# Two attention layers as steps of scores, transposes and products, with half projections between and SBUF shared out by phase

## The chip, the cores and the metric

The kernel runs on one core of a Trainium2 chip. The metric is device time in microseconds for one execution; the time before is the median of three runs, 1935.61 us (1925.61 to 1938.24). Lower is better.

## The reference, cut to what matters

Two trunk layers act on 512 latent tokens and 256 context tokens of width 1024, all in float32:

```python
for i in range(DEPTH):                       # DEPTH = 2
    h_l, h_c = modulate(rms_norm(x)), modulate(rms_norm(ctx))
    if kind == 0: y_l, y_c = diff_attention_mixer(h_l, h_c, ...)   # layer 0, 8 heads
    if kind == 1: y_l, y_c = neighbourhood_mixer(h_l, h_c, ...)    # layer 1, 16 heads
    x = x + mod_l[2] * y_l
    x = x + mod_l[5] * squared_relu_mlp(modulate(rms_norm(x)), w1, w2)
    # ctx likewise in layer 0 alone
```

Layer 0 is differential attention: per head two softmaxes over all keys are formed, the second is subtracted times lambda, and the result weighs the values; its output is normalised per head. Layer 1 is neighbourhood attention: a query sees the 256 context keys and a window of the grid, with a learned position bias added to the window's scores. Queries and keys are normalised per head; in layer 0 the latents also get a rotary embedding. The scales and shifts of each norm come from products of two conditioning vectors with a 1024 x 6144 matrix per layer ("modulation").

## The kernel before, in words

A token tile is 128 tokens; tiles 0 and 1 are context, 2 to 5 latents. A float32 matrix product is made of three passes over split operands (high and low part), each a matmul on float32r; every weight slice is therefore loaded raw (tag R, 2 buffers), copied to its high part by ScalarE (L99) and split by a subtraction on GpSimd (L100) into a W tile. `wload` does this (L90).

The program is a set of Python generators, each a stream of instructions that yields between steps. `run` (L796) steps them in the order that a string of letters gives: `q` projections, `a` the attention of the head before, `b` that of the head that is being projected, `l` and `m` load and compute one of 48 modulation chunks, a capital runs a stream to its end. What the strings give is the order in which instructions are written down; a scheduler in the framework then sets each engine's final order from its own estimate of times, taking earlier-written work first among what is ready.

Layer 0 (heads 1 to 7 in a loop of `hybrid_block`): `load_qkv` fetches four W tiles of the head; `qkv0` makes for each of six token tiles 24 matmuls of 384 columns into a PSUM tile PA (`qkv_matmul`, L346), normalises queries and keys (`qk_normed`: ScalarE copy and square, DVE reduction L358, epsilon added by `rstd` L231, power on GpSimd L233, DVE multiply L361), applies the rotary tables on GpSimd (L406 to L416), and after each pair of tiles transposes them (`turn`, L424, tile PC) and splits them (`q_split`, `k_split`; L385 is a DVE copy of the low key part to the other partition half). `attend0` then goes through the six query tiles. Per tile: scores into a three-bank PSUM tile PS (L458), maximum (L463), exponent (L464), the difference of the two softmaxes (L470), transposes of the weights into PB tiles (L478), high and low parts in an X tile (ScalarE L480, DVE L481), twelve products with the values (L485), the head norm (L488 to L494), and the transpose of the output (L446) one tile late. All of one query tile is one step of the stream.

PSUM in layer 0's attention holds PC once, PB twice, PA twice and PS once; in layer 1 PB twice, PS and PA three times. SBUF pools live for the whole program: W has 5 slots of 8 KB per partition, N has 4 of 4 KB, Y 7 of 1 KB. A head's four weight tiles and the next head's share the 5 slots of W.

Layer 1 has eight groups of two heads: `bias1` loads the position bias (six DMAs of 128 KB into an X tile, L514) and adds the mask on GpSimd (L517), `qkv1` projects, `attend1` makes four units per group (scores L575, bias L578, softmax L581 to L586, a copy of a straddling block L589, transposes L602, splits L603 and L604, products L612).

After each attention, `project` multiplies by the output matrix (L651); the first half of its columns goes beside the last head's attention. The MLPs (`mlp`: L719 up, L728 square, L730 and L731 split, L753 down, L764 sums) run after that.

## Time and profile before

| | before |
|---|---|
| median of 3 runs | 1935.61 us (1925.61 to 1938.24) |
| span of the profiled execution, first to last instruction | 1928.0 us |
| TensorE matmul (PE) busy | 1809.4 us, 94% |
| VectorE (DVE) busy | 1205.3 us, 63% |
| ScalarE (ACT) busy | 812.5 us, 42% |
| GpSimd (POOL) busy | 770.6 us, 40% |
| mean granted TensorE clock | 0.977 |
| HBM traffic | 95 GB/s over the span |

The profile is of one execution; its own total time is not recorded apart from the span, which lies 7.6 us under the median. PE is the row to read first, but matmuls overlap each other in the record, so "busy" also counts stretched matmuls: the spacing of matmuls in dense stretches tells more than the busy share. Waits are listed by who ended them. The stages can be told by their lines: layer 0's heads from about 92 to 445 us, its output projection to 560, its MLP to 1130, layer 1's groups from 1165 to 1490, its projection to 1560, its MLP to the end.

### The profile page before, as it was taken

The page shows a single profiled execution, that of the slowest core. Times are in us where ns is not written, and L with a number is a line of the kernel's source. Part 1 is how long each engine was busy: PE and PEld are TensorE (multiplying, and loading weights), DVE is VectorE, ACT ScalarE, POOL GpSimd, SP SyncE. Part 2 cuts the span into 40 slices and gives each one's busy share as a digit, 9 for nine tenths or more (in the row PEclk, how much of TensorE's full clock was granted, in tenths as well). Part 3 has the DMA queues.
Part 4 walks back from the last instruction along what each step waited for, and adds up shares of the span by engine and source line. Part 5 has one row for each costly group of instructions (what it writes and reads, how often), then busy time and mean ns, then how long its engine had stood idle before and what let it go on. Part 6 is the DMA issues. An engine that isn't in the chain of part 4 may idle for free.

```text
span 1928.0 us, 27111 instructions
## 1 busy us (share of the span) xinstructions
PE 1809.4 (94%) x10256; PEld 1574.1 (82%) x10256; DVE 1205.3 (63%) x2349; ACT 812.5 (42%) x1819; POOL 770.6 (40%) x620
## 2 busy tenths in 40 slices
PE   6899999997899999999999988998998989999998
PEld 5788888885688888888888968998897778888886
DVE  4688888887664343343334685988889664444447
ACT  4466666666342221221221244666656342232231
POOL 3655555544222221221222443444543334344443
PEclk9999999998999999999999998999998999999999
DMA  7222222225222332332432241223323223323331
GB/s 296 92 67 71 86 85 74 73 69 195 84 89 90 118 120 91 128 124 95 131 113 74 57 125 41 50 62 74 77 72 99 93 77 100 97 87 94 103 94 71
DMA packets 58723, 185.02 MB, mean 96 GB/s; under 512 B 7328, under 2 KB 13792, under 8 KB 54496
## 3 DMA queue, kind: packets, MB, share of 16 engines
q1 hardware_dynamic: 52848, 173.44, 29.1%
q10 hardware_dynamic: 5744, 9.85, 1.4%
q8 instruction: 80, 1.31, 0.3%
q14 instruction: 51, 0.42, 0.1%
HBM read 174.45 MB, written 8.81 MB: 95 GB/s over the span
## 4 chain that ended last, share of the span: by engine, by line
PE 67%; DVE 15%; DMA 6%; ACT 4%; POOL 4%; issue 4%; SPq 1%; ACTq 0%; POOLq 0%; DVEq 0%
PE PD L719 23%; PE PA L753 11%; PE PB L753 10%; PE PA L346 9%; PE PA L651 4%; PE PA L200 2%; DMA X<-in_rpb_dram 2%; PE PS L458 2%; PE PB L485 1%; POOL W L100 1%; PE PQ L335 1%; DVE SA L581 1%; DMA N<-oT 1%; DMA R<-in_wmod_dram 1%; DVE N L604 1%
## 5 line engine op out<-in xcount | busy, mean ns | idle before, releaser
L100 POOL TENSOR_TENSOR W<-R,W 128x1024 fp32r<-128x1024 f32 (+1 forms) x200 | 451.0, 2262 | 700.8 <-ACT W L99 700.7
L99 ACT ACTIVATE W<-R 128x1024 fp32r<-128x1024 f32 (+1 forms) x204 | 200.9, 994 | 457.8 <-PE PB L753 364.2
L719 PE MATMUL PD<-Q,W 128*128 128x384 f32 (+1 forms) x1584 | 291.4, 332 | 1.1 <-DVE Q L270 0.5
L719 PEld LDWEIGHTS PD<-Q,W 128*128 128x128 f32 x1584 | 269.5, 188 | 16.6 <-issue 7.0
L346 PE MATMUL PA<-W,H 128*128 128x384 f32 x1008 | 201.8, 347 | 5.1 <-DVE T L209 4.4
L728 DVE TENSOR_TENSOR N<-N 128x768 f32<-128x768 f32 (+1 forms) x64 | 61.9, 969 | 220.3 <-ACT N L727 110.7
L346 PE MATMUL PA<-W,Q 128*128 128x384 f32 (+1 forms) x1008 | 186.7, 332 | 10.9 <-DVE H L535 5.6
L719 PE MATMUL PD<-H,W 128*128 128x512 f32 (+1 forms) x816 | 187.6, 386 | 3.4 <-DVE H L271 2.5
L346 PEld LDWEIGHTS PA<-W,H 128*128 128x128 f32 x1008 | 176.3, 191 | 13.0 <-DVE T L209 4.9
L719 PEld LDWEIGHTS PD<-H,W 128*128 128x128 f32 x816 | 148.9, 191 | 36.3 <-DVE H L271 2.7
L346 PEld LDWEIGHTS PA<-W,Q 128*128 128x128 f32 x1008 | 162.7, 198 | 13.3 <-DVE H L535 7.0
L753 PE MATMUL PA<-W,H 128*128 128x512 f32 x648 | 168.1, 399 | 2.7 <-DVE T L759 2.5
L233 POOL TENSOR_TENSOR SQ<-SQ,half 128x4 f32<-128x4 f32 (+1 forms) x96 | 93.9, 979 | 161.0 <-DVE SQ L231 133.9
L753 PEld LDWEIGHTS PA<-W,H 128*128 128x128 f32 x648 | 119.2, 188 | 32.9 <-issue 6.2
L753 PE MATMUL PB<-W,H 128*128 128x512 f32 x504 | 132.3, 394 | 0.0
L753 PE MATMUL PA<-W,Q 128*128 128x512 f32 x432 | 108.7, 391 | 2.2 <-ACT Q L730 1.7
L753 PEld LDWEIGHTS PB<-W,H 128*128 128x128 f32 x504 | 94.5, 188 | 19.4
L764 DVE TENSOR_TENSOR H<-PA,H 128x512 f32<-128x512 f32 x78 | 53.7, 688 | 78.6 <-PE PA L753 78.6
L753 PEld LDWEIGHTS PA<-W,Q 128*128 128x128 f32 x432 | 80.9, 188 | 21.1 <-ACT Q L730 2.4
L464 ACT ACTIVATE E<-PS,SA 128x768 f32<-128x768 f32 (+1 forms) x96 | 72.7, 758 | 34.4 <-DVE SA L463 33.8
L463 DVE TENSOR_REDUCE SA<-PS 128x1 f32<-128x768 f32 (+1 forms) x96 | 74.4, 775 | 20.2 <-ACT E L464 13.6
L753 PE MATMUL PB<-W,Q 128*128 128x512 f32 x336 | 85.3, 389 | 0.0
(213 smaller groups left out, 3177.1 us busy)
## 6 DMA issues: line engine op xcount, KB each, us to landing
R<-in_w_dram SPq DMA_DIRECT2D x128, 512.0 KB
W<-in_wmod_dram SPq DMA_DIRECT2D x32, 1024.0 KB
R<-in_wmod_dram SPq DMA_DIRECT2D x32, 512.0 KB
R<-in_wqa_dram SPq DMA_DIRECT2D x32, 384.0 KB
R<-in_wqb_dram SPq DMA_DIRECT2D x32, 384.0 KB
X<-in_rpb_dram SPq DMA_DIRECT2D x48, 128.0 KB
R<-in_woa_dram SPq DMA_DIRECT2D x8, 512.0 KB
R<-in_wob_dram SPq DMA_DIRECT2D x8, 512.0 KB
```

Of the source, the lines that this page charges most:

```text
L99: nc.scalar.activation(w[:, 0, :n], raw, AF.Copy)
L100: (eng or nc.gpsimd).tensor_sub(w[:, 1, :n], raw, w[:, 0, :n].bitcast(F32))
L200: nc.tensor.matmul(ps[32 * q:32 * q + 32, 0:256], self.silu[:, kt, :], raws[kt], start=kt < 4, stop=kt >= 4)
L233: nc.gpsimd.tensor_tensor(r, ss, self.half[:, :n], op=ALU.pow)
L346: nc.tensor.matmul(acc[:, :n], hT[kt][:, x, P * i:P * i + P], w[kt // 2][:, y, o:o + n], start=(kt == 0 and p == 0), stop=(kt == KT - 1 an ...
L463: nc.vector.tensor_reduce(mx, s, op=ALU.max, axis=AX, negate=True)
L464: nc.scalar.activation(e[:, m, :nk], s, AF.Exp, bias=mx[:, 0:1], accum_out=sm[:, m:m + 1])
L651: nc.tensor.matmul(ps, oHL[h][:, x, c:c + P], w[h // 2][:, y, 512 * (h % 2):512 * (h % 2) + 512], start=(h == hs[0] and p == 0), stop=(h = ...
L719: nc.tensor.matmul(ps[:, at:at + b1 - b0], w[kt // 4][:, x, o:o + P], hT[kt][:, y, b0:b1], start=(kt == 0 and p == 0), stop=(kt == KT - 1 ...
L728: nc.vector.tensor_mul(r, r, r)
L753: nc.tensor.matmul(ps, hd[:, x, P * i - c0:P * i - c0 + P], w[f][:, y, 512 * n:512 * n + 512], start=(f == 0 and p == 0), stop=(f == len(h ...
L764: nc.vector.tensor_add(av, ps, av)
```

## The change

The arithmetic stays the same, and every engine's matmul work is the same set of instructions (9792 in the program on both sides). What changes:

1. **Steps.** `attend0` and `attend1` are cut into functions `scores`, `turned` (transposes and splits) and `weigh` (products and what follows), and tables `ATT0` and `ATT1` give their order: one tile's products are written down after the next tile's scores and a third tile's transposes.
2. **Half projections.** `qkv_matmul` makes half of a tile's 24 matmuls per call, with a step boundary between; `project`'s first part is halved too. The end of a head's projections (its last `turn`) is done in the next head's run, as stream `p`. In layer 1 the next group's first two token tiles are projected in the group before (stream `r`), and the bias of the next group is written down with its first scores (`b`) at the end of the group before.
3. **SBUF by phase.** W, N and a new tag OT become pools of a phase, of which five follow each other with four borders between (`sbuf_phase`): in layer 0's attention W has 8 slots of 6 KB and OT 2 of 3 KB; in layer 1's W has 6 slots of 6 KB and N 4 of 4 KB; elsewhere W 5 of 8 KB and N 4 of 4 KB as before. Y has 6 slots.
4. **Small operations.** The copy of the low key part goes from DVE to GpSimd (96 of them). Epsilon is summed by the reduction, from a 65th column of a constant tile `sq` into which the squares are written, so its DVE instruction goes in `qk_normed`. Four DVE operations with SBUF operands (L361, L494, L589, L731) become SCALAR_TENSOR_TENSOR with a factor of one.
5. **Modulation.** Four of layer 1's 24 chunks go from the first MLP to layer 1's last group and projection (`MODS_LATE`).

Core of the diff:

```diff
-ORD_HEAD = "qlalmqmaqqaqbqqbqaAQ"
-ORD_OUT0 = "lmlmaqaqaqAQ"
-ORD_GROUP = "qaqqaqaqaqAQ"
-ORD_OUT1 = "aqaqaqaAQ"
+ORD_HEAD = "aa qq aa q p q l a q a q m a l a qq a q aaa q m aaa qq a q b a q aa"
+ORD_OUT0 = "q l aaaa p a m l a m a q a q aaa q aaa qq a q a qq aa Q"
+ORD_GROUP = "qq a q a qq a a q a q a aa qqq a a r q a r b"
+ORD_GROUP7 = "qq a q a qq a a q a q a aa l qqq a a m q a b"
+ORD_OUT1 = "q a l a m a l aa m a q aa q a q a qq a l m Q"
+MODS_LATE = 4
+ATT0 = ((0, 1), (1, 0), (2, 0), (1, 1), (2, 1), (0, 2), (0, 3), (1, 2), (2, 2), (0, 4), (1, 3), (2, 3),
+        (0, 5), (1, 4), (2, 4), (1, 5), (2, 5))
+ATT1 = ((0, 1), (1, 0), (2, 0), (0, 2), (1, 1), (2, 1), (0, 3), (1, 2), (2, 2), (1, 3), (2, 3))
...
+    @contextmanager
+    def sbuf_phase(self, name, wcols, **tags):
+        with ExitStack() as st:
+            self.wcols, self.bufs = wcols, tags
+            self.room = {tag: st.enter_context(self.tc.tile_pool(name=name + tag, bufs=n, reuse_waits="tile"))
+                         for tag, n in tags.items()}
+            yield
...
-        acc = self.pst('A')
-        for kt in range(KT):
+        for kt in range(4 * half, 4 * half + 4):
...
-        nc.scalar.activation(sq, raw, AF.Square, scale=0.125)
+        nc.scalar.activation(self.sq[:, :ns, 0:64], xn, AF.Square, scale=0.125)
-        nc.vector.tensor_reduce(ss, sq.rearrange("p (a b) -> p a b", b=64), op=ALU.add, axis=AX)
-        r = self.rstd(ss, ns, 'SQ')
-        nc.vector.tensor_mul(xn, xn,
-                             r[:, :, None].to_broadcast([P, ns, 64]))
+        nc.vector.tensor_reduce(ss, self.sq[:, :ns], op=ALU.add, axis=AX)
+        r = self.power(ss, ns, 'SQ')
+        nc.vector.scalar_tensor_tensor(xn, xn, 1.0, r[:, :, None].to_broadcast([P, ns, 64]),
+                                       op0=ALU.mult, op1=ALU.mult)
...
-            nc.vector.tensor_copy(kl[b, m, cols], kl[a, m, cols].bitcast(F32))
+            nc.gpsimd.tensor_copy(kl[b, m, cols], kl[a, m, cols].bitcast(F32))
...
+        soft, wTs = {}, {}
+        scores(0)
+        yield
+        for stage, i in ATT0:
+            (scores, turned, weigh)[stage](i)
             yield
...
-                nc.vector.tensor_sub(u[:, 1, :], r, u[:, 0, :].bitcast(F32))
+                nc.vector.scalar_tensor_tensor(u[:, 1, :], r, 1.0, u[:, 0, :].bitcast(F32),
+                                               op0=ALU.mult, op1=ALU.subtract)
...
+        big, small = dict(wcols=1024, W=5, N=4), dict(wcols=768, W=8, OT=2)
...
+            ph.close()
+            ph.enter_context(b.sbuf_phase("sA", **small))
...
+            ph.close()
+            ph.enter_context(b.sbuf_phase("sB", **big))
...
+        ph.enter_context(b.sbuf_phase("sC", wcols=768, W=6, N=4))
...
+            ph.enter_context(b.sbuf_phase("sD", **big))
```

Where it moves instructions, at the three places of which the prediction speaks. The lines of the changed kernel are its own: L516 is the transpose of L478, L527 the product of L485, L370 the projection of L346, L492 the scores of L458, L235 a modulation product of L213, L117 the weight split of L100, L112 the raw weight load of L95, L563 the bias load of L514, L407 the key copy of L385.

TensorE in layer 0, one query tile of a middle head, before: PB652 and PB653 take the two halves of the transposed weights E644, from which X651 is made; PB654 takes its products.

```order
L478 MATMUL PB652_3049<-ident_69,E644_3026 128x128 x3
L346 MATMUL PA789_3669<-W782_3657,H83_453 128x384 x2
L346 MATMUL PA789_3669<-W782_3657,H84_460 128x384 x3
L346 MATMUL PA789_3669<-W784_3662,H94_542 128x384
L478 MATMUL PB653_3055<-ident_69,E644_3026 128x128 x3
L485 MATMUL PB654_3061<-Q484_2298,X651_3048 128x256 x9
L200 MATMUL PA814_3776<-R794_3707,silu_84 32x256 x4
L346 MATMUL PA789_3669<-W784_3662,H94_542 128x384 x2
```

And now, for a query tile of the same kind (PB710 and PB711 from E680, X709, products in PB716):

```order
L516 MATMUL PB710_3450<-ident_66,E680_3313 128x128 x3
L516 MATMUL PB711_3456<-ident_66,E680_3313 128x128 x3
L370 MATMUL PA793_3804<-W728_3531,H83_460 128x384
L370 MATMUL PA793_3804<-W728_3531,H84_467 128x384
L235 MATMUL PA781_3762<-sel_73,T782_3771 128x2 x2
L370 MATMUL PA793_3804<-W728_3531,H84_467 128x384 x2
L370 MATMUL PA793_3804<-W730_3536,H94_549 128x384 x2
L492 MATMUL PS733_3541<-Q596_2892,Q595_2891 128x256
L492 MATMUL PS733_3541<-Q597_2893,Q595_2891 128x256
...
L370 MATMUL PA793_3804<-W730_3536,H95_556 128x384 x3
L527 MATMUL PB716_3489<-Q448_2217,X709_3449 128x256 x12
```

Before, the products follow the second transposes at once; now ten projection matmuls, four scores and two small ones stand between. At some tiles the old order is still there, as at this earlier one of the same head (X668 is made of PB669 and PB670):

```order
L516 MATMUL PB669_3248<-ident_66,E639_3107 128x128 x3
L516 MATMUL PB670_3254<-ident_66,E639_3107 128x128 x3
L527 MATMUL PB674_3287<-Q448_2217,X668_3247 128x256 x6
```

Here nothing stands between the transposes and the products.

SyncE's DMA queue in layer 1, around the bias of a middle group (X2192 and X2288), before:

```order
L95 DMA R2173_11893<-in_wqb_dram 128x768
L514 DMA X2192_11956<-in_rpb_dram 128x1x256 x2
L95 DMA R2175_11898<-in_wqb_dram 128x768
L514 DMA X2192_11956<-in_rpb_dram 128x1x256 x2
L95 DMA R2177_11903<-in_wqb_dram 128x768
L514 DMA X2192_11956<-in_rpb_dram 128x1x256 x2
```

And now (X2119 is the bias of the group ahead of the one whose weights R2037 to R2043 are):

```order
L563 DMA X2119_11828<-in_rpb_dram 128x1x256 x4
L112 DMA R2037_11351<-in_wqb_dram 128x768
L563 DMA X2119_11828<-in_rpb_dram 128x1x256 x2
L112 DMA R2039_11356<-in_wqb_dram 128x768
L112 DMA R2041_11361<-in_wqb_dram 128x768
L112 DMA R2043_11366<-in_wqb_dram 128x768
```

The bias pieces stood between weight loads, one load ahead of every two pieces; now all but two stand ahead of them.

GpSimd in layer 0 now, where the last keys of a head (Q891) are copied; before, these copies stood on DVE:

```order
L117 TENSOR_TENSOR W1020_4875<-R1019_4873,W1020_4875 128x768
L117 TENSOR_TENSOR W1022_4880<-R1021_4878,W1022_4880 128x768
L407 CAST Q891_4243<-Q891_4243 64x256
L258 TENSOR_TENSOR SQ988_4719<-SQ987_4717,half_79 128x4
L407 CAST Q891_4243<-Q891_4243 64x256
L258 TENSOR_TENSOR SO868_4186<-SO866_4182,half_79 128x1
L117 TENSOR_TENSOR W1024_4885<-R1023_4883,W1024_4885 128x768
```

The copies stand between weight splits of the next head and powers, in one queue with them.

271 lines of the change are left out of this document (163 added, 108 removed).

## The prediction

> **What bounds the kernel now.** I read the stages first (the view that sums each engine's busy time over stretches). Columns are the stretch and its length in us, then busy us and instruction counts of PE, its weight loads, DVE, ACT and POOL, then the granted clock share, the DMA share and GB/s.
>
> ```profile
> 92.00:445.00 353.00, 326.59 (x2156) 293.80 (x2154) 292.00 (x695) 234.54 (x671) 187.36 (x228) 0.99 0.25 80
> 445.00:560.00 115.00, 101.71 (x469) 80.10 (x470) 73.73 (x148) 52.20 (x124) 34.00 (x24) 0.91 0.31 101
> 560.00:1130.00 570.00, 566.66 (x3166) 492.19 (x3166) 254.79 (x343) 135.97 (x183) 169.34 (x79) 1.00 0.33 107
> 1165.00:1490.00 325.00, 298.82 (x1988) 287.26 (x1988) 272.57 (x654) 198.07 (x507) 140.59 (x147) 0.95 0.26 68
> 1490.00:1560.00 70.00, 62.24 (x307) 50.75 (x305) 46.35 (x83) 30.79 (x61) 23.91 (x17) 0.95 0.27 87
> 1560.00:1928.00 368.00, 358.14 (x1588) 292.94 (x1588) 184.13 (x235) 102.07 (x134) 152.10 (x66) 0.99 0.30 92
> ```
>
> The MLPs (560 to 1130, 1560 to the end) leave PE idle for 3.3 and 9.9 us: nothing of this change can give much there. The heads of layer 0 (92 to 445) leave 353.0 - 326.6 = 26.4 us idle, the groups of layer 1 (1165 to 1490) 26.2, the two projections 13.3 and 7.8. In layer 1's groups DVE is busy for 272.6 of 325 us, 84%, and in layer 0's heads for 292.0 of 353, 83%: it is the second engine that could bind.
>
> A busy PE is not a dense PE, so I price the matmuls of layer 0's heads at their spacing in dense stretches, from the chain of work that ended last (start, us, what, count):
>
> ```profile
> 401.59 1.00 PE PA L200 x16
> 406.41 0.55 PE PA L205 x2
> 408.21 1.41 PE PS L458 x8
> 416.17 0.33 PE PB L478 x3
> 420.54 1.45 PE PB L485 x12
> 422.10 4.40 PE PA L346 x25
> ```
>
> That is 62 ns per modulation matmul, 275 for L205, 176 for a score, 110 for a transpose, 121 for a product, 176 for a projection. The counts, and PE's idle time by who ended it, stand in the groups by line and shape of 92 to 445 us:
>
> ```profile
> L346 PE MATMUL PA<-W,H 128*128 128x384 f32 x937 | 186.2, 345 | 1.9 <-DVE T L209 1.6 <-POOL W L100 0.2
> L485 PE MATMUL PB<-Q,X 128*128 128x256 f32 x368 | 58.1, 297 | 11.4 <-DVE X L481 7.4 <-ACT X L480 3.6 <-DVE SO L231 0.4
> L458 PE MATMUL PS<-Q,Q 128*128 128x512 f32 x108 | 34.9, 404 | 1.1 <-ACT E L464 1.0
> L478 PE MATMUL PB<-ident,E 128*128 128x128 f32 x184 | 30.5, 276 | 2.7 <-DVE O L489 1.8 <-ACT N L447 0.9
> L458 PE MATMUL PS<-Q,Q 128*128 128x256 f32 x168 | 28.1, 288 | 0.0
> L200 PE MATMUL PA<-R,silu 128*32 128x256 f32 x224 | 17.1, 388 | 7.1 <-DMA R<-in_wmod_dram 5.3 <-DVE Y L361 1.8
> L424 PE MATMUL PC<-ident,Y 128*128 128x128 f32 x84 | 14.7, 282 | 0.5 <-ACT Q L384 0.4
> L446 PE MATMUL PB<-ident,O 128*128 128x128 f32 x39 | 10.7, 275 | 0.0
> L213 PE MATMUL PA<-sel,T 128*128 128x2 f32 x32 | 4.2, 237 | 0.5 <-ACT T L203 0.5
> L205 PE MATMUL PA<-T,sel 128*32 128x256 f32 x12 | 3.7, 391 | 1.2 <-ACT T L203 1.2
> ```
>
> 937 x 0.176 + 368 x 0.121 + 276 x 0.176 + 307 transposes x 0.110 + 224 x 0.062 + 32 x 0.110 + 12 x 0.275 = 164.9 + 44.5 + 48.6 + 33.8 + 13.9 + 3.5 + 3.3 = 312.5 us. So of 353 us some 40.5 are lost, 26.4 as idle and 14 as matmuls that run stretched around the waits: **each microsecond of idle stands for 1.53 lost**. I use that factor for layer 1 too, an estimate: 26.2 x 1.53 = 40 us, where the clock of 0.95 in its row (0.05 x 325 = 16 us at a lowered clock) is part of it.
>
> Who waits: L485, the products, wait 11.4 us for the split of their own weights, and modulation products wait 8.8 (L200, L205, L213). One place, in order of time on PE and then on SyncE's queue (what released it in brackets):
>
> ```profile
> 275.68 0.51 PE L478 MATMUL PB<-ident,E 128*128 128x128 f32 x3
> 277.99 1.33 PE L485 MATMUL PB<-Q,X 128*128 128x256 f32 x9 [1.80 <-DVE X L481]
> 282.44 0.64 PE L200 MATMUL PA<-R,silu 128*32 128x256 f32 x8 [1.01 <-DMA R<-in_wmod_dram]
> ```
> ```profile
> 193.13 26.19 SPq L95 DMA_DIRECT2D R<-in_wqa_dram  x4
> 222.28 8.91 SPq L113 DMA_DIRECT2D R<-in_wmod_dram  x4
> ```
>
> The products stand directly behind the transposes and wait 1.80 us. Four weight loads of one head take 26 us to issue, since a raw buffer comes free only when its split has a W slot, and W has one spare slot; the modulation loads queue behind them.
>
> **The change, part by part.**
>
> *Steps in layer 0.* The new order puts ten projections and four scores between transposes and products where none stood. The split behind them takes an ACT copy and a DVE subtraction; 1.80 us of wait behind 0 us of cover says what is needed, and 10 x 0.176 + 4 x 0.12 is 2.2 us. But the order shows tiles with no cover still (PB674): about five of 42 in the heads against eight with at most a pair of projections before. I take L485's 11.4 us to 4. Ends: 0 and 11.4.
>
> *W with 8 slots.* The next head's four splits no longer wait for the last projection of this head, so the loads of 26 us spread into the head before, and modulation loads land earlier; their products are also written later after their load. L200, L205 and L213: 8.8 to 1.5. The transposes' 2.7 us (PB has two tiles as before, waits for L489) I leave at 2.5; L346 goes from 1.9 to 1, scores and L424 from 1.6 to 2 (the key copies, below). Idle 26.4 to 11: **15.4 x 1.53 = 23.6 us**.
>
> *Layer 1's groups.* The rows with idle there:
>
> ```profile
> L346 PE MATMUL PA<-W,Q 128*128 128x256 f32 x336 | 53.5, 315 | 10.9 <-DVE H L535 5.6 <-ACT H L384 3.1 <-POOL W L100 2.0
> L575 PE MATMUL PS<-H,H 128*128 128x256 f32 x244 | 49.7, 303 | 3.8 <-DVE H L375 1.5 <-ACT E L582 1.3 <-ACT H L384 0.6
> L602 PE MATMUL PB<-ident,E 128*128 128x128 f32 x224 | 37.3, 287 | 3.5 <-DVE T L618 3.4
> L612 PE MATMUL PB<-N,H 128*128 128x256 f32 x168 | 35.9, 303 | 2.5 <-DVE N L604 1.3 <-ACT N L603 1.0
> L542 PE MATMUL PA<-ident,Y 128*128 128x128 f32 x32 | 9.0, 282 | 4.1 <-DVE Y L361 4.0
> L544 PE MATMUL PA<-ident,Y 128*128 128x128 f32 x48 | 12.1, 272 | 1.1 <-DVE Y L361 1.1
> ```
>
> The waits of L346 and L542 are for DVE and POOL work at the start of a group (evacuations, the norm's multiply, weight splits). The first two token tiles now come a group early, the bias loads stand ahead of the weight loads, W has a second spare slot, and DVE has less to do. L346 10.9 to 4, L542 and L544 from 5.2 to 2, L602 to 1, L612 to 2; L575 stays at 4, since the scores still follow the key transposes directly in some groups. Idle 26.2 to 13.3: **12.9 x 1.53 = 19.7 us**.
>
> *DVE and POOL.* The rows of the whole program (mean ns after the busy us):
>
> ```profile
> L385 DVE CAST Q<-Q 64x256 fp32r<-64x256 f32 x48 | 24.1, 503 | 1.5
> L385 DVE CAST H<-H 64x256 fp32r<-64x256 f32 x48 | 18.3, 382 | 1.5
> L231 DVE TENSOR_SCALAR SQ<-SQ 128x4 f32<-128x4 f32 x80 | 22.9, 286 | 1.3
> L470 DVE SCALAR_TENSOR_TENSOR E<-E,SA 128x768 f32<-128x768 f32 x32 | 33.3, 1041 | 0.7
> L731 DVE TENSOR_TENSOR H<-N,H 128x768 fp32r<-128x768 f32 x32 | 53.8, 1685 | 13.9 <-ACT H L730 13.8
> L556 POOL CAST V<-H 64x256 fp32r<-64x256 f32 x16 | 6.9, 431 | 27.4 <-PE PB L612 21.5 <-DVE H L535 5.4
> ```
>
> DVE loses 24.1 + 18.3 + 22.9 = 65 us, nearly all in the two attentions. With the forecast stretches of 329 and 305 us its share is (292.0 - 24.1 - 11.5) / 329 = 78% and (272.6 - 18.3 - 11.5) / 305 = 80%. That is cover for the gains above and no term of its own. POOL takes 96 copies at 0.43 us, 41 us; with 187.4 + 42 x 0.43 = 205 us of 353 in layer 0 it stays under 65% busy. The price of a copy that queues behind one weight split is bounded by nothing (the scores need it later) and 1.9 us; the 0.4 us that I added to the scores is near the lower end, because now some matmuls lie between the last key transposes and the scores in layer 0. A SCALAR_TENSOR_TENSOR of 768 columns takes 1041 ns, a TENSOR_TENSOR of 768 columns 1685 beside the weight splits. At the end of each MLP, where the last split is waited for, I take 1 us each: **2 us**; elsewhere PE covers it.
>
> The Trainium skill, "SBUF — State Buffer", section "SBUF: two separate sides", says that DVE and GpSimd share a port pair under an exclusive lock, and counts every DVE operation with two SBUF inputs among those that lose it to a GpSimd operation that reads SBUF. By that rule the new form, which has two SBUF inputs, gains nothing, and these 2 us fall away; the row of L470, 1041 ns with two SBUF inputs beside the same GpSimd work, speaks against it.
>
> *Modulation late.* Four chunks leave the first MLP, at 16 x 62 ns + 4 x 110 ns = 1.4 us each, 5.7 us on a PE that has no idle there; in layer 1's last group and projection (7.8 us idle) about 2 come back. Their loads become 8 instead of 4 on SyncE, in a queue that moves 68 GB/s there. **4 us.**
>
> *Projections.* 13.3 + 7.8 us of idle. The start waits for all of a head's projections, since the split outputs take the buffers of the normalised tokens, and this order is the same now; only the output weights load before the modulation chunks. **5 us**, ends 0 and 12.
>
> *SBUF rooms, halves.* No instructions are added. At each of the four borders a new tile waits for the tiles that lay there; before, it waited for a slot of the same pool, which came free at the same time. A projection in halves holds its PA tile longer; I cost both at nothing, because the scheduler puts other work of PE there, and give the price without that cover as a rival.
>
> Sum: 23.6 + 19.7 + 2 + 4 + 5 = 54 us, rounded to 55. Against the profiled execution: 1928 to 1873. The median lies 7.6 us above that span, so **1880.6 us**.
>
> **Rivals.**
>
> *B: PSUM binds, not the order.* PB stays at two tiles, of which each query tile takes four in turn, and PS at one. Then products and transposes wait as before in both layers, and only the modulation waits, (8.8 - 1.5) x 1.53 = 11.2 us, and the MLPs' 4 and 2 us go: 17 us, 1918. For it: L478's waits for L489 are waits for a PB tile. Against it: most of L485's 11.4 us was for X, not for PB. The Trainium skill, "Perfetto Trace Analysis", section "Optimization Strategy", says that the same gap again and again can mean too little SBUF or PSUM for the next tile; that speaks for this case as to PSUM, and for the forecast as to W.
>
> *C, slower: the rooms.* If at a border the new room's loads wait for the whole old room, each border costs a serial load of a weight set:
>
> ```profile
> 433.03 19.15 SPq L95 DMA_DIRECT2D R<-in_woa_dram  x6
> ```
>
> 19 us at each of the four borders is 76 us: 1880.6 + 76 = 1957. It decides from 14 us a border on. Against it: waits are kept per tile, and the slots under the new tiles are mostly those of the head before.
>
> *D: the attentions become dense.* All of 40.5 and 40 us comes back, with 15 elsewhere: 1840. For it: DVE at 80% and POOL under 65%. Against it: uncovered tiles in the new order.
>
> **How the numbers follow.** Forecast 0.62, B 0.18, D 0.14, C 0.06. A change of about 1% (19 us) can just be told from none. Faster by over 1% means under 1916: the forecast, D, and a third of B, 0.82; within 1% two thirds of B, 0.12; slower 0.06. The range takes D's end and B's: 1840 to 1918. C and the half of B that is slower than its price lie outside, some of D below it too.
>
> **What would show it.** Right: L485's successor (L527) with under 5 us of idle in layer 0's heads, L222's waits for the modulation loads gone, layer 1's clock near 0.98, and the two stretches at about 329 and 305 us. Wrong: idle moved to the scores (L492, L632) with POOL's key copy as releaser, to the first loads after a border, or to transposes that wait for PB.

## The result, and the profile after

| | before | changed |
|---|---|---|
| median | 1935.65 us (1925.61 to 1938.24, 4 runs) | 1956.83 us (1950.85 to 1959.31, 4 runs) |
| ratio, with 95% interval | | 1.0117 (1.0095 to 1.0139) |
| span of the profiled execution | 1928.0 us | 1957.5 us |

The change made the kernel 21 us slower; 55 us faster was forecast, and the result lies outside the range. The profiled execution of before lies under its median, and that of the changed kernel is the slowest of its four, so the two traces are 29.5 us apart. Both hold the same number of matmul records, 10256.

The stretches of the changed kernel first, in the view of busy time by stretch, with the same columns as ahead of the prediction:

```profile
92.00:465.00 373.00, 342.59 (x2163) 302.77 (x2162) 273.57 (x607) 233.19 (x667) 218.30 (x275) 0.96 0.25 79
465.00:586.00 121.00, 105.93 (x520) 84.14 (x519) 76.97 (x154) 53.48 (x132) 33.46 (x26) 0.90 0.29 100
...
1184.00:1490.00 306.00, 289.44 (x1983) 279.51 (x1983) 236.55 (x553) 190.09 (x498) 152.59 (x190) 0.98 0.27 67
1490.00:1590.00 100.00, 77.80 (x380) 58.06 (x378) 55.66 (x94) 38.76 (x74) 34.26 (x22) 0.82 0.39 122
```

Layer 0's heads take 373 us where they took 353, and their granted clock went from 0.99 to 0.96. Layer 1's groups take 306 instead of 325, which is close to the forecast of 305. What lies between those groups and the last MLP grew from 70 to 100 us, at a clock of 0.82.

Stretches that are cut at round times can blur such a comparison, so I also cut at fixed instructions on PE: the first matmul of each head's projections, of the output projection, and of the MLPs. "First head" is layer 0's head 1, "to MLP" runs from the last projection matmul of a layer to the first one of its MLP. Times in us, of the profiled executions:

| kernel | first head | heads 2 to 7 | to MLP 0 | MLP 0 | groups | to MLP 1 | MLP 1 |
|---|---|---|---|---|---|---|---|
| before | 44.9 | 314.6 | 134.9 | 606.0 | 300.2 | 88.7 | 367.2 |
| changed | 54.2 | 326.4 | 141.0 | 598.2 | 281.3 | 119.1 | 367.2 |
| difference | +9.3 | +11.8 | +6.1 | -7.8 | -18.9 | +30.4 | 0 |

So two forecast gains came, in the first MLP and in the groups, and 58 us were lost in four other places. Three of them lie right behind a border between two SBUF rooms.

**Layer 0's heads.** PE's groups by line and shape from 92 to 465 us; the last numbers are PE's idle time ahead of them and who ended it:

```profile
L370 PE MATMUL PA<-W,H 128*128 128x384 f32 x954 | 188.4, 345 | 2.5 <-DVE Q L423 2.4
L527 PE MATMUL PB<-Q,X 128*128 128x256 f32 x356 | 57.3, 301 | 7.9 <-DVE X L519 7.3 <-DVE O L531 0.6
L492 PE MATMUL PS<-Q,Q 128*128 128x512 f32 x111 | 39.6, 438 | 2.4 <-ACT E L498 2.3
L516 PE MATMUL PB<-ident,E 128*128 128x128 f32 x178 | 29.8, 280 | 9.1 <-ACT OT L481 5.9 <-DVE O L531 2.4 <-DVE E L504 0.7
L222 PE MATMUL PA<-R,silu 128*32 128x256 f32 x232 | 23.2, 391 | 0.0
L445 PE MATMUL PC<-ident,Y 128*128 128x128 f32 x84 | 16.8, 304 | 4.9 <-ACT Q L406 4.4 <-POOL Y L437 0.5
```

The modulation products (L222) wait no longer, where 7.1 us were; with the small products behind them (L227 and L235, before L205 and L213) 8.8 us went to 1.8, and 1.5 was forecast. The products with the values (L527) went from 11.4 to 7.9 and not to 4. The transposes (L516) wait 9.1 us where 2.7 were: 8.3 of them for L481 and L531, which empty a PB tile. The transposes of queries and keys (L445), which share the one PC tile, went from 0.5 to 4.9. All idle together is 373.0 - 342.6 = 30.4 us against 26.4 before. Four us of idle do not make 20 us; a good part of the rest is in the clock. One place shows how. PE in order of time, then the busy time of the same stretch in pieces of 2 us (the clock is the third number from the end):

```profile
188.88 0.51 PE L527 MATMUL PB<-Q,X 128*128 128x256 f32 x3
189.79 0.62 PE L527 MATMUL PB<-Q,X 128*128 128x256 f32 x3 [0.40 <-DVE X L519]
190.25 0.27 PE L480 MATMUL PB<-ident,O 128*128 128x128 f32 x1
191.16 0.55 PE L516 MATMUL PB<-ident,E 128*128 128x128 f32 x3 [0.64 <-ACT OT L481]
192.28 0.55 PE L516 MATMUL PB<-ident,E 128*128 128x128 f32 x3 [0.57 <-DVE O L531]
193.72 2.83 PE L527 MATMUL PB<-Q,X 128*128 128x256 f32 x12 [0.89 <-DVE X L519]
```

```profile
190.00:192.00 2.00, 1.06 (x7) 0.59 (x6) 1.94 (x5) 1.67 (x4) 0.36 (x2) 1.00 0.00 0
192.00:194.00 2.00, 0.83 (x5) 0.60 (x6) 1.95 (x4) 1.92 (x8) 0.90 (x2) 0.96 0.01 4
194.00:196.00 2.00, 2.00 (x11) 2.00 (x11) 1.53 (x6) 1.58 (x4) 0.95 (x2) 0.50 0.01 4
196.00:198.00 2.00, 2.00 (x11) 1.76 (x11) 1.47 (x4) 0.77 (x3) 0.00 (x0) 0.68 0.00 0
```

There is attention only, no projection: each of three small groups waits for the one before to pass through DVE and ACT, which are nearly full (1.94 and 1.67 of 2 us). No wait is longer than 0.89 us, but PE is busy for 1.89 of 4 us, and the clock granted right behind it is 0.50. The twelve products then take 2.83 us; twelve took 1.45 in the chain of before. The trace has such half-clock pieces of 3.4 us or a multiple. In heads 2 to 7 the changed kernel has five, before one: 5 x 3.4 / 2 = 8.5 us of matmul time lost against 1.7. With 2.7 us more of idle there (23.3 against 20.6) that is 9.5 of the 11.8 us. Over the whole program their length follows from the mean clock:

```profile
core 0: 1957.5 us, clock 0.965
```

(1 - 0.965) x 1957.5 / 0.5 = 137 us at half clock, against (1 - 0.977) x 1928.0 / 0.5 = 89 us before. Half of the difference is 24 us of matmul work, at most, since PE is idle in a part of these pieces. The Trainium skill, "TensorE: Matmul & The Clock Gate", section "A second HAM failure mode: psum-queue depth-cycling", says that a kernel which cycles through its PSUM tiles can idle briefly between groups of matmuls so often that the clock swings between half and full; this trace agrees, with 0.50 behind waits of 0.40 to 0.89 us.

**The borders.** SyncE's queue ahead of the first head, what it waited for (us in total, times, longest), and PE where the head's first weights arrive, before:

```profile
46.87 9.69 SPq L95 DMA_DIRECT2D R<-in_wqa_dram  x3
```

```profile
SPq L95 <- POOL W L100: 13.9, 3, 6.5
```

```profile
66.65 4.48 PE L346 MATMUL PA<-W,H 128*128 128x384 f32 x24 [0.43 <-DVE Q L402]
```

And in the changed kernel (L360 are the last projections of head 0, which read W tiles of the old room):

```profile
45.25 24.73 SPq L112 DMA_DIRECT2D R<-in_wqa_dram  x3
```

```profile
SPq L112 <- POOL W L117: 28.9, 3, 22.0
```

```profile
59.80 3.81 PE L360 MATMUL PQ<-W,H 128*128 128x384 f32 x21
67.72 5.60 PE L370 MATMUL PA<-W,H 128*128 128x384 f32 x22 [1.97 <-POOL W L117]
```

Three raw weight loads take 24.73 us to issue where they took 9.69, and one raw buffer is held for 22.0 us by a split (L117) whose W tile lies in the new room; before, the longest such wait was 6.5 us. On ScalarE, no weight is copied into a W tile (L116) between 43.3 and 64.19 us: the copies go on 0.6 us after head 0's last product, at 63.61, has read the old room. Before, five of them start between 44 and 61 us. Head 1's projections then wait for their own weights, which they did not do before. Behind layer 1 the output projection's loads wait too, SyncE first, then its waits, then PE:

```profile
1495.96 1.74 SPq L736 DMA_DIRECT2D N<-oT  x4
1507.44 11.33 SPq L130 DMA_DIRECT2D R<-in_wmod_dram  x5
```

```profile
SPq L112 <- PE PA L222: 33.0, 2, 26.1
SPq L736 <- DVE N L664: 16.8, 1, 16.8
```

```profile
1508.88 1.20 PE L677 MATMUL PB<-N,H 128*128 128x256 f32 x4 [7.61 <-DVE N L664]
1512.02 1.08 PE L222 MATMUL PA<-R,silu 128*32 128x256 f32 x8 [1.95 <-DMA R<-in_wmod_dram]
```

The outputs of the other heads (L736) wait 16.8 us for N tiles, and the attention's products wait 7.61 us for the split into theirs (L664). An output weight waits 26.1 us for a raw buffer that a late modulation chunk holds; but that wait ended at 1468.4 us, ahead of the others, and is not the border's: in the kernel one_room below, without borders, it is 28.6 us, while L736 waits 2.1 us at the longest and the products of layer 1's last run 1.5 us in all, against 8.9 here.

### The profile page after: what moved, and what is told of

Its sections match the earlier page's. It is cut to its first block, busy times and chain, and to the rows that moved or that the text cites. A ratio compares the mean times of both kernels' runs of the same rounds, so it can differ in the third digit from the quotient of the medians.

```text
span 1957.5 us, 27066 instructions
## 1 busy us (share of the span) xinstructions
PE 1823.7 (93%) x10256; PEld 1585.6 (81%) x10256; DVE 1158.9 (59%) x2159; ACT 809.1 (41%) x1819; POOL 817.1 (42%) x716
## 3 DMA queue, kind: packets, MB, share of 16 engines
q1 hardware_dynamic: 53424, 173.44, 28.6%
## 4 chain that ended last, share of the span: by engine, by line
PE 73%; DVE 10%; ACT 5%; DMA 5%; POOL 4%; issue 3%; SPq 0%; ACTq 0%; POOLq 0%; DVEq 0%
PE PD L794 22%; PE PA L370 13%; PE PA L829 11%; PE PB L829 10%; PE PA L723 5%; PE PA L222 3%; PE PB L527 2%; PE PS L492 1%; PE PQ L360 1%; PE PB L677 1%; POOL W L117 1%; PE PS L632 1%; PE PB L662 1%; ACT W L116 1%; ACT E L498 1%
## 5 line engine op out<-in xcount | busy, mean ns | idle before, releaser
L117 POOL TENSOR_TENSOR W<-R,W 128x1024 fp32r<-128x1024 f32 (+1 forms) x200 | 453.3, 2275 | 669.8 <-ACT W L116 668.6
L116 ACT ACTIVATE W<-R 128x1024 fp32r<-128x1024 f32 (+1 forms) x204 | 200.3, 994 | 453.0 <-PE PB L829 374.8
L370 PE MATMUL PA<-W,H 128*128 128x384 f32 x1008 | 201.6, 348 | 8.8 <-DVE Q L423 4.9
L370 PEld LDWEIGHTS PA<-W,H 128*128 128x128 f32 x1008 | 177.7, 193 | 18.3 <-issue 6.5
L370 PE MATMUL PA<-W,Q 128*128 128x384 f32 (+1 forms) x1008 | 180.3, 325 | 3.6 <-DVE H L582 3.2
L370 PEld LDWEIGHTS PA<-W,Q 128*128 128x128 f32 x1008 | 158.1, 191 | 4.7 <-DVE H L582 3.9
L829 PEld LDWEIGHTS PA<-W,Q 128*128 128x128 f32 x432 | 81.2, 188 | 22.2 <-ACT Q L805 2.4
```

The lines of the kernel that those rows point to most:

```text
L116: nc.scalar.activation(w[:, 0, :n], raw, AF.Copy)
L117: (eng or nc.gpsimd).tensor_sub(w[:, 1, :n], raw, w[:, 0, :n].bitcast(F32))
L370: nc.tensor.matmul(acc[:, :n], hT[kt][:, x, P * i:P * i + P], w[kt // 2][:, y, o:o + n], start=(kt == 0 and p == 0), stop=(kt == KT - 1 an ...
L829: nc.tensor.matmul(ps, hd[:, x, P * i - c0:P * i - c0 + P], w[f][:, y, 512 * n:512 * n + 512], start=(f == 0 and p == 0), stop=(f == len(h ...
```

## The experiments

My theory at that point had three parts: the small steps make layer 0's tiles wait for each other's PSUM tiles; the borders delay the loads behind them; the late chunks hold up the last projection. The rivals were the key copies in GpSimd's queue, and the late chunks or the order of the last run alone. "Before" ran beside each group of kernels, at 1931 to 1935 us.

### One part undone at a time

**l0_old.** Layer 0 and its output projection in the old order, all else as changed (core of the edit; whole projections are written in one step again):

```diff
-ORD_HEAD = "aa qq aa q p q l a q a q m l a qq a q aaa q m aaa qq a q b a q aa"
+ORD_HEAD = "qlalmqmaqqaqbqqbqaAQ"
...
-        for stage, i in ATT0:
-            (scores, turned, weigh)[stage](i)
+        for i in range(NT):
+            scores(i)
+            turned(i)
+            weigh(i)
             yield
```

> The changed kernel with layer 0's attention and its output projection written in the order of before (whole query tiles, whole projections, the old strings of letters); rooms, small operations, late modulation and all of layer 1 stay as changed. Theory 1 (the separated steps hold PSUM tiles longer, so transposes and key transposes wait): the stretch from the first to the last head projection goes from 380.6 us back to about 358, the transposes' idle for a free PB tile nearly goes, and the time is about 1957 - 22 - 9 = 1926 us. Theory 2 (rooms or small operations cost it): the stretch stays near 380 and the time near 1957.

**mods0.** No late chunks:

```diff
-MODS_LATE = 4
+MODS_LATE = 0
-ORD_GROUP7 = "qq a q a qq a a q a q a aa l qqq a a m q a b"
-ORD_OUT1 = "q a l a m a l aa m a q aa q a q a qq a l m Q"
+ORD_GROUP7 = "qq a q a qq a a q a q a aa qqq a a q a b"
+ORD_OUT1 = "q a a a aa a q aa q a q a qq a Q"
```

> The changed kernel with all modulation chunks in the first MLP again (none in layer 1's last group and projection). Theory 1 (the late chunks' loads and their raw buffers hold up the output weights): the time from layer 1's last projection to the first output product goes from 52 us to about 32, the second output weights load some 20 us earlier, the first MLP gains nothing back beyond 6 us, and the time is 1957 - 25 + 6 = 1938 us. Theory 2 (the order of the last projection's steps, or the new room, is what costs): 52 us stay within 5, and the time is 1955 to 1963.

**one_room.** The four borders are taken out, the first room serves the whole program:

```diff
-            ph.close()
-            ph.enter_context(b.sbuf_phase("sA", **small))
...
-                oTs.append(self.sbt('OT' if last is None else 'N', [P, T]))
+                oTs.append(self.sbt('N', [P, T]))
```

> The changed kernel with one SBUF room for the whole program as before (W 5 of 8 KB, N 4 of 4 KB, the outputs in N); steps, small operations and late modulation as changed. Theory 1 (each border delays the first loads behind it: the first head by 9 us, the two projections by 5 to 14): the first layer-0 head goes from 54.2 us back to about 45, the raw weight loads ahead of it from 24.7 to about 10, and the time is 1957 - 9 - 14 = 1934 us, if five W slots cost the other heads nothing. Theory 2 (the eight W slots earn more than the borders cost): heads 2 to 7 get slower than 326 us, and the time is 1957 or more.

**l0old_one** puts the three together, and **l0old_late** is the same with the late chunks kept.

> Layer 0's attention and output projection in the order of before, no late modulation, one room; kept of the change are layer 1's steps, half projections and early first tiles, and the small operations. If the parts found so far add up (layer 0's steps 13 us, borders 9 + 14, late chunks 16 - 6), the time is 1957 - 13 - 23 - 10 = 1911 us, below both kernels; layer 1's groups stay at about 281 us. If layer 1's gain needs its room, with six W slots, groups go back towards 300 and the time to 1930.

> Layer 0 in the order of before, one room, layer 1's steps, small operations, and the four late modulation chunks kept. If the late chunks cost 17 us in layer 1's projection by themselves, the time is 1920 + 17 - 6 = 1931 us. If they cost that only behind the border, where weights, outputs and their raw loads wait for the same slots, layer 1's last run loses about 2 us by them and the first MLP keeps 6: 1916 us, below both kernels.

| kernel | median, us | ratio to before | first head | heads 2 to 7 | to MLP 0 | MLP 0 | groups | to MLP 1 |
|---|---|---|---|---|---|---|---|---|
| changed | 1956.83 | 1.0117 (1.0095 to 1.0139) | 54.2 | 326.4 | 141.0 | 598.2 | 281.3 | 119.1 |
| l0_old | 1943.24 | 1.0056 (1.0037 to 1.0075) | 54.2 | 313.4 | 138.2 | 595.8 | 279.9 | 120.4 |
| mods0 | 1948.84 | 1.0067 (1.0052 to 1.0082) | 53.9 | 324.4 | 142.6 | 603.6 | 280.7 | 102.5 |
| one_room | 1940.79 | 1.0042 (1.0029 to 1.0056) | 47.5 | 319.7 | 142.0 | 598.7 | 284.4 | 103.9 |
| l0old_one | 1920.25 | 0.9939 (0.9918 to 0.9960) | 41.6 | 315.6 | 134.2 | 605.3 | 280.4 | 101.4 |
| l0old_late | 1921.35 | 0.9930 (0.9909 to 0.9951) | 42.4 | 315.0 | 132.5 | 598.2 | 285.8 | 105.4 |

These stretches are of one execution each. In the three kernels with the changed layer 0 (changed, mods0, and out1_a below) heads 2 to 7 take 324.4 to 326.4 us, in the six with that of l0old_one 315.0 to 317.7, so 2 to 3 us there tell nothing. Between the changed kernel and one_room the two profiled executions differ by 23 us, the medians by 16.

Undone alone, layer 0's order gives 14 us, the rooms 16, the late chunks 8; undone together they give 37 (by the ratios to the "before" that ran beside each: 12, 15, 10 and 34). The signs were as expected, the times were not: 1926, 1934, 1938 and 1911 us had been expected of the four. l0old_one beats both kernels: before by 0.6% (0.4 to 0.8). That the three add up is partly chance. In the last run the rooms and the late chunks share one loss: taking out either gives 15 or 16.6 us there (119.1 to 103.9 or 102.5), taking out both no more (101.4). In one room the late chunks cost nothing in the whole (1921.35 against 1920.25): they lose 9 us in the last group and run and win 7 in the first MLP. The rooms and the order, for their part, are worth more together at the first head (54.2 to 47.5 without rooms, to 41.6 with the old order too). In heads 2 to 7 the rooms cost 7 us with the new order (326.4 against 319.7) and nothing with the old one (313.4 against 315.6); why is open. In one_room, the raw loads ahead of the first head and its first projections are back where they were:

```profile
46.88 9.68 SPq L112 DMA_DIRECT2D R<-in_wqa_dram  x3
```

```profile
66.58 7.23 PE L370 MATMUL PA<-W,H 128*128 128x384 f32 x40 [0.44 <-DVE Q L423]
```

### What in layer 0's order costs

**psum3.** One set of three PSUM tiles for transposes, products and key transposes:

```diff
-PS_ATTN0 = dict(C=1, B=2, A=2, S=1)
+PS_ATTN0 = dict(B=3, A=2, S=1)
...
-            ps = self.pst('A' if accs else 'C')
+            ps = self.pst('A' if accs else 'B')
```

> The changed kernel with layer 0's single PC tile and two PB tiles made one set of three, for transposes, products and key transposes. Theory 1 (the count of PSUM tiles binds the separated steps): the transposes' and key transposes' lost time in the heads, 14 and 8 us, about halves, and the time is about 1946 us. Theory 2 (the latency from the transposes through ACT and DVE binds, not the count): within 4 us of 1957.

1980.33 us, ratio 1.0234 (1.0219 to 1.0249); heads 2 to 7 take 345.7 us. Neither theory said that. PE's groups from 92 to 484 us:

```profile
L527 PE MATMUL PB<-Q,X 128*128 128x256 f32 x356 | 60.3, 303 | 7.9 <-DVE X L519 4.2 <-ACT X L518 3.7
L492 PE MATMUL PS<-Q,Q 128*128 128x512 f32 x108 | 42.1, 475 | 23.8 <-ACT E L498 23.8
L516 PE MATMUL PB<-ident,E 128*128 128x128 f32 x184 | 29.5, 287 | 0.0
L445 PE MATMUL PB<-ident,Y 128*128 128x128 f32 x76 | 11.4, 272 | 0.0
```

The waits for a PB or the PC tile are gone (9.1 and 4.9 us to nothing), so they came from how three tiles were shared out. But the scores now wait 23.8 us for the single PS tile. PE in order of time at one such place:

```profile
182.37 0.99 PE L492 MATMUL PS<-Q,Q 128*128 128x256 f32 x5
187.45 2.93 PE L492 MATMUL PS<-Q,Q 128*128 128x512 f32 x8 [4.09 <-ACT E L498]
```

Scores now stand right behind the last ones, whose exponents ACT still reads from the one tile. The wait was moved to the next scarce tile.

Four kernels take the new order apart, each a small edit of the changed kernel. **att_seq** writes the table `ATT0` in tile order, (1, 0), (2, 0), (0, 1), (1, 1), (2, 1) and so on. **whole_proj** writes the 24 matmuls of a projection together:

```diff
-            acc = self.pst('A')
             for half in range(2):
-                self.qkv_matmul(acc, half, w, hT, i, 0, 384)
                 if half == 1:
+                    acc = self.pst('A')
+                    self.qkv_matmul(acc, 0, w, hT, i, 0, 384)
+                    self.qkv_matmul(acc, 1, w, hT, i, 0, 384)
                     tile_(i, acc)
```

**no_ahead** drops `p` from `ORD_HEAD` and ends it with one `q` more. **att_whole** takes the table of att_seq and writes a query tile as one step at the place of its scores:

```diff
-            (scores, turned, weigh)[stage](i)
+            if stage == 0:
+                scores(i)
+                turned(i)
+                weigh(i)
```

**att_whole_one** is att_whole in one room without late chunks.

> The changed kernel with the table of layer 0's steps in tile order: scores, transposes, products of one tile, then those of the next; half projections and strings of letters as changed. Theory 1 (that two tiles are under way at a time makes them wait for each other's PSUM tiles): heads 2 to 7 go from 326 to about 315 us, the time to 1945. Theory 2 (the half projections and the strings cost it): heads stay at 326 and the time within 5 us of 1957.

> The changed kernel, but a layer-0 projection's 24 matmuls are written together, at the place of the second half. Theory H (a tile in halves holds one of two PA tiles longer, which the modulation and the next projection need): heads 2 to 7 go from 326 to about 316 us, the time to 1947. Theories P and S: 326 and 1957 within 4 us, or above, since less work stands between dependent steps.

> The changed kernel, but a layer-0 head's last key transposes are written at the end of its own run again, not in the next head's (stream p gone). Theory P (the last keys come late, and the next head's attention waits for them): layer 0's heads 2 to 7 go from 326 to about 316 us and the time from 1957 to 1947. Theory H (half projections) or S (steps smaller than a tile): 326 and 1957 within 4 us.

> The changed kernel, but a query tile of layer 0 is written as one step, at the place of its scores, with half projections, strings and stream p kept. Theory S (the steps set the other streams' work between a tile's transposes and products, and its PB tiles are held over them): heads 2 to 7 go from 326 to about 316 us, the time to 1947. Theories H and P: 326 and 1957 within 4 us, or above.

> One room, no late chunks, layer 1 as changed, layer 0 with half projections, strings and the end of a head's projections in the next run, but each query tile one step at the place of its scores. If the steps smaller than a tile were all that was wrong in layer 0, heads 2 to 7 take about 314 us and the time is 1920 as with the order of before; if the eight W slots or the strings matter too, heads 2 to 7 take 320 us or more and the time is 1926 or more.

PE's idle time and the loss at half clock (half the length of these pieces) are of heads 2 to 7; before takes 314.6 us there, with 20.6 and 1.7, l0_old 313.4, with 19.5 and 0.

| kernel | median, us | ratio to before | heads 2 to 7 | PE idle | loss at half clock | to MLP 0 |
|---|---|---|---|---|---|---|
| changed | 1956.83 | 1.0117 (1.0095 to 1.0139) | 326.4 | 23.3 | 8.5 | 141.0 |
| att_seq | 1960.26 | 1.0139 (1.0118 to 1.0161) | 327.0 | 22.4 | 10.2 | 140.4 |
| whole_proj | 1954.92 | 1.0102 (1.0077 to 1.0127) | 324.8 | 25.3 | 8.5 | 144.5 |
| no_ahead | 1958.23 | 1.0120 (1.0099 to 1.0141) | 322.7 | 24.5 | 1.7 | 140.4 |
| att_whole | 1952.68 | 1.0097 (1.0070 to 1.0123) | 316.4 | 20.8 | 0 | 144.7 |
| att_whole_one | 1929.32 | 0.9963 (0.9949 to 0.9978) | 312.0 | 20.6 | 0 | 137.3 |

att_seq fells the theory as I had put it: with one tile after the other the heads stay at 327 us, so it is not two tiles under way that collide. Half projections and the late end of a head's projections are not it either. Only whole tiles, the one thing in which att_whole differs from att_seq, take the heads to 316, and in one room to 312, less than before's 314.6. att_whole has its transposes' waits back at 3.8 us and no half-clock piece in heads 2 to 7 (PE's groups from 92 to 457 us, then the same twelve products as above):

```profile
L527 PE MATMUL PB<-Q,X 128*128 128x256 f32 x356 | 54.8, 292 | 9.8 <-DVE SO L252 4.6 <-DVE X L519 3.2 <-ACT X L518 1.8
L516 PE MATMUL PB<-ident,E 128*128 128x128 f32 x178 | 29.2, 284 | 3.8 <-DVE O L531 2.7 <-ACT OT L481 1.1
```

```profile
197.14 1.60 PE L527 MATMUL PB<-Q,X 128*128 128x256 f32 x12
```

So the steps smaller than a tile cost 10 us in the heads, 8.5 of them by the clock and 2.5 by idle time. The two nearly account for every kernel: heads 2 to 7 less PE's idle time less the loss at half clock are 291 to 297 us in all twenty. The strings put several of the steps in a row without a projection between ("aaa"), as in the place shown, and there PE is busy for less than half of the time and the clock falls. That a projection between every two steps would mend it, no run shows.

When the clock falls can be read from the traces (all but that of key_dve, whose clock is odd, see the end). The half-clock pieces of a trace begin and end on one grid of 3.41 us. Of the windows of this grid from 66 to 1900 us that ran at full clock, in 19 traces, 173 had PE busy for under 45%, and half clock followed all of them; with 45% to 75% it followed 105 of 576, with more none of 8901. In heads 2 to 7 the changed kernel has five windows under 45%. No_ahead has one, and six others at 55% to 59%; att_whole has none, with its lowest at 55%. So about the same idle time costs the clock or not by how it falls on the windows, and that no_ahead has a single piece may be luck of this kind. Its whole time is no shorter.

In the whole time att_whole wins 4 us, and the intervals overlap: the last head's attention, which no projections follow, takes 4 us more on the way to the MLP. Att_whole_one has the shortest heads of all, but takes 9 us more than l0old_one: its first head takes 48.5 us against 41.6, the stretch to MLP 0 137.3 against 134.2, and the groups, where the two kernels are the same, 285.1 against 280.4. That the heads' own edit (10 us) and the whole of layer 0's old order (13 us) differ by 3 us is hardly more than the spread.

### Layer 1 and its last run

**out1_a** is mods0, and **out1_one** is l0old_one, with the projection's first step later in the last run. **l1_no_early** is l0old_one without early tiles, **l1_whole** is l0old_one with a unit as one step, and **l1whole_out1** has the edits of out1_one and l1_whole:

```diff
-ORD_OUT1 = "q a a a aa a q aa q a q a qq a Q"
+ORD_OUT1 = "aaa q aaa q aa q a q a qq a Q"
...
-ORD_GROUP = "qq a q a qq a a q a q a aa qqq a a r q a r b"
+ORD_GROUP = "qq qq a q a qq a a q a q a aa qqq a a q a b"
...
-            (scores, turned, weigh)[stage](u)
+            if stage == 0:
+                scores(u)
+                turned(u)
+                weigh(u)
```

> All modulation in the first MLP, and in layer 1's last run the projection's first step (weights and outputs loaded) written after three steps of the attention instead of ahead of it, the second after six. If the loaded outputs hold the N slots that the attention's transposed weights need, the products' and transposes' lost time there (21 us) falls by about 8, and the time from the last projection of layer 1 to the second MLP from 102.6 to about 95 us; the whole 1949 - 8 = 1941 us. If the border is what holds the slots, it stays within 3 us of 102.6.

> As the kernel with layer 0 as before, one room and no late chunks, with the last run's order in which the projection's first step stands after three steps of the attention. If the order costs there with one room as well, the stretch behind the groups goes from 101 to about 96 us and the time to 1915; if loads are early anyway with one room, 101 and 1920 within 3.

> As the kernel with layer 0 as before, one room and no late chunks (1920 us, groups 280 us, from there to the second MLP 101 us), but no token tile of layer 1 is projected a group early. If the early tiles make the groups dense and take cover from the last run, the groups go to about 292 us and the stretch behind them to about 92: 1922 us together. If the steps make the gain, the groups stay at about 281 and the stretch behind them falls: 1912 us.

> As the kernel with layer 0 as before, one room and no late chunks, but each unit of layer 1's attention is one step again, at the place of its scores; early tiles and half projections kept. If the steps make the gain of 19 us in the groups, they go back to about 295 us and the time to 1934; if the early tiles make it, the groups stay within 4 us of 280 and the time near 1920.

> As the kernel with layer 0 as before, one room and no late chunks, with each unit of layer 1's attention as one step and the projection's first step behind the first unit of the last run. If the two savings add, the stretch behind the groups goes to about 93 us and the time to 1915; if both saved the same waits, 97 and 1919.

| kernel | median, us | ratio to before | groups | to MLP 1 |
|---|---|---|---|---|
| mods0 | 1948.84 | 1.0067 (1.0052 to 1.0082) | 280.7 | 102.5 |
| out1_a | 1941.89 | 1.0050 (1.0030 to 1.0070) | 280.6 | 98.9 |
| l0old_one | 1920.25 | 0.9939 (0.9918 to 0.9960) | 280.4 | 101.4 |
| out1_one | 1918.07 | 0.9920 (0.9897 to 0.9944) | 282.3 | 94.5 |
| l1_no_early | 1925.90 | 0.9963 (0.9946 to 0.9980) | 286.7 | 101.5 |
| l1_whole | 1918.95 | 0.9920 (0.9898 to 0.9942) | 284.0 | 97.2 |
| l1whole_out1 | 1919.61 | 0.9938 (0.9917 to 0.9960) | 283.5 | 97.6 |

The early tiles are worth 6 us in the groups, and the last run does not pay for them (101.5 against 101.4). The steps are worth 3.6 us in the groups and give 4.2 back in the last run: nothing. The order of the last run gives 4 to 7 us at its place; of the whole, out1_a is 7 us below mods0, while in one room it cannot be told from none. Four kernels lie at 1918 to 1920 us, and their differences are no wider than their runs.

### The key copies

**key_dve** puts the 96 copies of the changed kernel back on DVE, **l0old_keydve** those of l0old_one:

```diff
-            nc.gpsimd.tensor_copy(kl[b, m, cols], kl[a, m, cols].bitcast(F32))
+            nc.vector.tensor_copy(kl[b, m, cols], kl[a, m, cols].bitcast(F32))
```

> The changed kernel with the 96 key copies on DVE again. If the copies in GpSimd's queue are what delays scores and key transposes in layer 0 (10 and 8 us lost there), the time falls to about 1940 us; if the steps' order is the cause, it stays within 5 us of 1957, rather above, since DVE has 42 us of work more.

> As the kernel with layer 0 as before, one room and no late chunks (1920 us), but the key copies on DVE again. If the copies on GpSimd made a part of the gain, layer 1's groups go from 280 to about 287 us, layer 0's heads from 357 to about 360, and the time to 1930; if DVE's load does not bind once the order is as before, all stays within 3 us.

key_dve takes 1973.83 us, ratio 1.0199 (1.0184 to 1.0215): 17 us more than the changed kernel, so the rival that the copies in GpSimd's queue do harm falls by the sign. l0old_keydve takes 1936.10, ratio 1.0018 (0.9999 to 1.0037): 16 us more than l0old_one, of them 8 in layer 0's heads (365.3 against 357.2 us) and 5 in layer 1's groups (285.6 against 280.4). The copies on DVE in key_dve:

```profile
L407 DVE CAST Q<-Q 64x256 fp32r<-64x256 f32 x48 | 17.9, 374 | 1.5
L407 DVE CAST H<-H 64x256 fp32r<-64x256 f32 x48 | 16.3, 339 | 1.5
```

These are 34 us of DVE's time, and half of that is time of the kernel: DVE is on the path in places. Heads 2 to 7 are not one of them in the changed kernel's order (325.8 us with the copies on DVE, 326.4 without); there the groups (288.2 against 281.3) and the stretches to the two MLPs (144.7 against 141.0, 122.0 against 119.1) are longer. Both runs put the copies back with the rest of the change in place. That the copies alone would gain 16 us on the kernel before, no run shows: without the copies on GpSimd, all else that l0old_one keeps is worth nothing that can be told from before, though the early tiles alone gave 6 us; layer 0's heads then take 365.3 us against before's 359.5 in nearly the same order. What costs them that was not tried.

## Why the prediction was wrong, point by point

1. **Steps in layer 0, 11.4 to 4 us, in a term of 23.6 us.** This is the main step that failed; the heads lost 21.1 us. The waits of the products fell to 7.9 only. The prediction counted five tiles of 42 without cover, against eight with at most a pair of matmuls before. By the profiles, 16 tiles had at most two matmuls between transposes and products before, and 9 still have none; these 9 wait 7.2 of the 9.2 us that the products wait in the runs of heads 1 to 7. And 24 of the 42 had five or more matmuls between already before. "The transposes' 2.7 us (PB has two tiles as before, waits for L489) I leave at 2.5" was wrong: 9.1. I had named PSUM as a rival and put a price of nothing gained on it, not of a loss. In the first head the border costs 7 us with the new order (13 with the old). In heads 2 to 7 whole tiles give 10 us back and one room alone 7, of 11.8 lost, so these overlap. What the steps brought there in place of the gain is 8.5 us at half clock and 2.5 us of idle time.
2. **"Each microsecond of idle stands for 1.53 lost."** With about the same dense work, 312.5 us, 373 - 312.5 = 60.5 us are lost over 30.4 of idle, a factor of 2.0. The factor is not a constant: 20.8 us of idle came with no loss at half clock in att_whole, and 23.3 with 8.5 us in the changed kernel. Idle time and clock had to be priced apart.
3. **W with 8 slots.** The modulation products' waits went nearly as forecast, 8.8 to 1.8. But "At each of the four borders a new tile waits for the tiles that lay there; before, it waited for a slot of the same pool, which came free at the same time" was the second step that failed: with a free slot of the old pool there was nothing to wait for. The rooms cost 16 us in all. That is rival C's mechanism at a fifth of its price: behind the first border 6.7 us and behind layer 1 15.2 (with the late chunks), ahead of the first output projection 0 to 4 (142.0 in one_room; with the old order 138.2 against 134.2), into layer 1 nothing. That C's 1957 is what was measured is chance.
4. **Layer 1's groups, 19.7 us.** 18.9 came, by other causes than mine. PE's groups from 1184 to 1490 us:

```profile
L370 PE MATMUL PA<-W,Q 128*128 128x256 f32 x336 | 47.0, 292 | 3.6 <-DVE H L582 3.2 <-ACT H L406 0.4
L662 PE MATMUL PB<-ident,E 128*128 128x128 f32 x220 | 34.7, 282 | 4.7 <-DVE T L683 4.7
L677 PE MATMUL PB<-N,H 128*128 128x256 f32 x162 | 34.3, 297 | 4.2 <-ACT N L663 2.1 <-DVE N L664 1.9
L591 PE MATMUL PA<-ident,Y 128*128 128x128 f32 x48 | 12.5, 273 | 0.8 <-DVE Y L383 0.8
```

   The projections' waits fell from 10.9 to 3.6 (forecast 4) and those of the query and key transposes from 5.2 to 1.6, L591's row and as much at L589 (forecast 2): here the early tiles show, 6 us. The steps' part did not come: L662 and L677 went from 3.5 and 2.5 to 4.7 and 4.2, where 1 and 2 were forecast. The key copies made 5 to 7 us of the gain. The rest, 6 to 8 us, no run tells apart; the steps may have 3.6 of it.
5. **"That is cover for the gains above and no term of its own"**, on DVE's load. With the rest of the change in place the copies are worth 16 us, its largest gain. At 83% and 84% of the stretch DVE was said to be "the second engine that could bind", and then was not priced. Its share fell to 273.6 / 373 = 73% and 236.6 / 306 = 77% (forecast 78% and 80%).
6. **The split of the MLP as SCALAR_TENSOR_TENSOR, 2 us.** Nothing came. DVE's rows of the whole program:

```profile
L806 DVE SCALAR_TENSOR_TENSOR H<-N,H 128x768 fp32r<-128x768 f32 x32 | 52.2, 1635 | 14.1 <-ACT H L805 14.1
L806 DVE SCALAR_TENSOR_TENSOR Q<-N,Q 128x512 fp32r<-128x512 f32 x32 | 47.0, 1472 | 12.6 <-ACT Q L805 11.6
L536 DVE SCALAR_TENSOR_TENSOR O<-O,SO,one 128x128 f32<-128x128 f32 x48 | 31.1, 650 | 12.5 <-POOL SO L258 12.2
L646 DVE SCALAR_TENSOR_TENSOR E<-E,one 128x64 f32<-128x64 f32 x32 | 8.2, 256 | 0.2
```

   1635 ns against 1685 at 768 columns, 1.6 us in all 32, and even that is not the form's: in the nine kernels that have the new form but no late chunks it takes 1688 or 1689 ns. The rule that the prediction weighed, in the Trainium skill's "SBUF — State Buffer", section "SBUF: two separate sides", counts every DVE operation with two SBUF inputs among those that contend with a GpSimd operation that reads SBUF. The time agrees with it, since both forms have two such inputs and take the same; that the port is the reason, no run shows. The row of L470 that I held against it was no test, since it stood in another stretch, beside other work of GpSimd.
7. **Modulation late, 4 us.** The first MLP gave 5.4 us (603.6 in mods0 against 598.2); the last run took 16.6 behind the border.
8. **Projections, 5 us.** They lost 6.1 and 30.4: the first by the rooms and the order together (134.2 in l0old_one), the second by the late chunks behind the border (16.6), by the order of the last run (4 to 7), and 6 or more by what I leave open. "This order is the same now" overlooked that the new strings begin with the projection's loads, so that in layer 1 these and the attention's transposed weights ask for the same four N tiles.

Of the signs for "right", the end of L222's waits, layer 1's clock (0.98) and its stretch (306 us) showed, L527 under 5 us and the stretch of layer 0 did not. Of those for "wrong", the transposes that wait for PB and the first loads behind a border showed, the key copies as releaser did not.

## What to carry to other kernels

A second engine at 83% is a term, not cover: with 34 us of small copies back on it, the kernel takes 16 us more. A room of its own for each phase can cost a load's lead at its border (7 and 15 us at two of the four here), so put a border where the next phase's first loads are not wanted at once. Cutting a step finer did not help here, since other work did not come between the pieces everywhere; several small dependent pieces in a row left PE busy for less than half of a 3.41-us window, and the clock behind them halved. Price idle time and the clock apart.
